# The last feed-forward's second product by Strassen's seven half-block products, token-major

## The chip, the core and the metric

The kernel runs on one core of a Trainium2 chip. Its engines work side by side, each through its own instructions in their order: TensorE (PE, with its weight loads as PEld), VectorE (DVE), ScalarE (ACT), GpSimd (POOL); SyncE (SP) issues most of the loads and stores. The metric is the device time of one execution in microseconds (us), median of several. The span is the time from the first to the last instruction of one profiled execution.

## What is computed

Two transformer-like blocks follow each other on x of 512 tokens by 1024 channels, in fp32. The last step of the second block is the part that is changed; all else (projections, a state-space scan, window attention, a first feed-forward, a recurrent mixer, latent attention, cross attention to a memory) stays.

```python
def rmsnorm_2(x, g):
    xf = x.astype(jnp.float32)
    y = xf * lax.rsqrt(jnp.mean(xf * xf, axis=-1, keepdims=True) + EPS)
    return (y * g.astype(jnp.float32)).astype(x.dtype)
...
        h = rmsnorm_2(x, norm_ffn_g[l])
        x = x + jnp.square(jax.nn.relu(h @ w_ff1[l])) @ w_ff2[l]
    return x
```

w_ff1 is 1024 by 4096, w_ff2 is 4096 by 1024. The factor 1/rms of a token goes through relu and square as 1/rms squared, so the kernel multiplies the result of the second product by 1/(mean of squares + EPS), a number for each token, and uses h without that factor.

## The kernel before

Matrices are held with 128 rows on the partitions. Each fp32 factor of a large product is split into two parts of a narrower type (fp32r): hi, a cast on ScalarE, and lo, source minus hi, on VectorE. A product is three matmuls: hi by hi, lo by hi, hi by lo. Weights come in units of 1 MB (class `Unit`): `load` issues the DMA on SyncE's queue into `raw` (two buffers), `split` makes `whi` (L140) and `wlo` (L141), two buffers each, in two halves of 128x1024. `use(key)` splits the unit that is used and the next one in the stream, and loads the one after that; so the casts of a unit wait until TensorE has read the last matmul of the unit two places ahead of it.

The last feed-forward is `mlp(1, ...)`. It goes over the 4096 hidden channels in four quarters q. In a quarter the first product (keys "f1", four units) makes 8 tiles of 128 hidden channels by 512 tokens, each of 24 matmuls of 128x512 (L267 to L269 of the helper `cm`; the first two units of the first quarter through `cm4`, L1024 to L1026). `f_evac` takes a tile out of PSUM: relu and square on ScalarE (into `ua_h`), the same square in full precision on GpSimd (`fsq`, L1166) and the difference on VectorE (`ua_l`, L1167). The second product (keys "f2", four units) makes 8 tiles of 128 output channels by 512 tokens, each of 24 matmuls again, through two PSUM banks (tag "g") in turn. In the first three quarters its sums gather in `acc` in SBUF; in the last, `fin2` multiplies by the factor of each token (`rb`, spread over the partitions by `bcast_tokens`, L337, from `token_sums`, L330), adds the residual `xT` (channels on the partitions), and `out_channels` turns each finished tile by four transposes (L1703), copies it and stores it token-major.

A scheduler of the framework sets each engine's order within the limits of the data; the engines then keep that order. What sets the order by hand are the lines of `use`, `ahead` and `cm`. The first feed-forward, `mlp(0, ...)`, uses the same function.

## Time and profile before

| | us |
|---|---|
| median of three runs | 1928.96 (1928.72 to 1932.59) |
| the profiled execution's own time | 1931.84 |
| its span | 1930.1 |
| TensorE busy | 1867.0 (97%) |
| VectorE busy | 1046.5 (54%) |
| ScalarE busy | 886.8 (46%) |
| GpSimd busy | 480.3 (25%) |
| mean granted clock of TensorE | 0.994 of full speed |

Busy times are of one profiled execution. Matmuls are pipelined: one of 128x512 shows some 0.39 us from its start to its modelled end, while the next one starts some 0.23 us after it. A wait's releaser is the engine and line that ended it. The difference of 1.74 us between the execution's time and its span lies around the span.

### The profile page before, as it was taken

The numbers are of one execution on the slowest core, as the hardware profiler recorded it, in microseconds if no ns is written. First come the engines' busy times: TensorE is split into PE (matmuls) and PEld (weight loads), VectorE is DVE, ScalarE is ACT, GpSimd is POOL, SyncE is SP. The second block draws the span as 40 slices with busy tenths as digits, with TensorE's granted clock in tenths as the row PEclk, the third lists the DMA queues.
The fourth block names the chain that finished last, engine by engine and source line by source line (L and its number), as shares of the span: only waits on it lengthen the run. The fifth ranks groups of instructions, "written<-read, shape, count | busy, mean of one in ns | idle before, by whom it ended". The sixth has DMA issues, their size and how long they took to land. (4 is left out here: it accounts for less than half of the span.)

```text
span 1930.1 us, 24665 instructions
## 1 busy us (share of the span) xinstructions
PE 1867.0 (97%) x9685; PEld 1541.7 (80%) x9685; DVE 1046.5 (54%) x1687; ACT 886.8 (46%) x1461; POOL 480.3 (25%) x530
## 2 busy tenths in 40 slices
PE   8899999999999999998999999989999999999999
PEld 7788888888887777886888888887867778888887
DVE  6767762666456653547233334667567763333543
ACT  6656663766435664345332323444453543323231
POOL 1454441444202321234021202322111431101020
PEclk9999999999999999999999999999999999999999
DMA  5222112222232222332323223322112213332322
GB/s 170 73 68 68 55 59 88 67 68 63 84 96 83 65 74 88 124 118 93 115 87 111 97 88 109 97 77 68 51 44 66 87 44 109 100 97 88 108 88 66
DMA packets 169378, 164.11 MB, mean 85 GB/s; under 512 B 8742, under 2 KB 165101, under 8 KB 169262
## 3 DMA queue, kind: packets, MB, share of 16 engines
q1 hardware_dynamic: 157322, 151.03, 24.9%
q10 hardware_dynamic: 9444, 9.89, 1.6%
q0 software_dynamic: 2496, 1.61, 0.4%
q8 instruction: 76, 1.25, 0.3%
q14 instruction: 40, 0.33, 0.1%
HBM read 158.26 MB, written 4.23 MB: 84 GB/s over the span
## 5 line engine op out<-in xcount | busy, mean ns | idle before, releaser
L141 DVE TENSOR_TENSOR wlo<-raw,whi 128x1024 fp32r<-128x1024 f32 (+2 forms) x285 | 368.1, 1305 | 272.5 <-ACT whi L140 263.2
L140 ACT CAST whi<-raw 128x1024 fp32r<-128x1024 f32 (+2 forms) x285 | 288.1, 1031 | 412.5 <-PE psg L268 387.8
L267 PE MATMUL psg<-hh,whi 128*128 128x512 f32 (+1 forms) x1016 | 404.0, 398 | 0.8 <-DVE hl L319 0.8
L268 PE MATMUL psg<-hl,whi 128*128 128x512 f32 (+1 forms) x1016 | 401.1, 395 | 0.0
L269 PE MATMUL psg<-hh,wlo 128*128 128x512 f32 (+1 forms) x1016 | 398.8, 393 | 0.0
L267 PE MATMUL psg<-ua_h,whi 128*128 128x512 f32 x800 | 316.5, 396 | 0.5 <-DVE xT L1564 0.5
L268 PE MATMUL psg<-ua_l,whi 128*128 128x512 f32 x800 | 313.4, 392 | 0.0
L269 PE MATMUL psg<-ua_h,wlo 128*128 128x512 f32 x800 | 312.3, 390 | 0.0
L267 PEld LDWEIGHTS psg<-hh,whi 128*128 128x128 f32 (+1 forms) x1016 | 191.0, 188 | 40.7 <-issue 1.2
L269 PEld LDWEIGHTS psg<-hh,wlo 128*128 128x128 f32 (+1 forms) x1016 | 191.0, 188 | 40.0
L268 PEld LDWEIGHTS psg<-hl,whi 128*128 128x128 f32 (+1 forms) x1016 | 191.0, 188 | 38.6 <-DVE hl L316 0.4
L1166 POOL TENSOR_TENSOR fsq<-relu 128x512 f32<-128x512 f32 x64 | 80.9, 1265 | 508.1 <-ACT relu L1163 477.6
L267 PEld LDWEIGHTS psg<-ua_h,whi 128*128 128x128 f32 x800 | 150.0, 188 | 35.3 <-DVE xT L1564 2.4
L268 PEld LDWEIGHTS psg<-ua_l,whi 128*128 128x128 f32 x800 | 150.3, 188 | 32.4 <-DVE ua_l L1167 1.2
L269 PEld LDWEIGHTS psg<-ua_h,wlo 128*128 128x128 f32 x800 | 150.2, 188 | 30.8
L285 PE MATMUL psg<-whi,hh 128*128 128x256 f32 x416 | 122.5, 295 | 10.6 <-ACT cacc L571 3.6
L286 PE MATMUL psg<-wlo,hh 128*128 128x256 f32 x416 | 120.4, 289 | 1.0 <-DVE wlo L141 1.0
L287 PE MATMUL psg<-whi,hl 128*128 128x256 f32 x416 | 120.7, 290 | 0.0
L988 POOL TENSOR_TENSOR ssq<-ssq,sq 128x512 f32<-128x512 f32 x42 | 66.5, 1583 | 117.2 <-ACT sq L987 116.1
L285 PEld LDWEIGHTS psg<-whi,hh 128*128 128x128 f32 x416 | 80.4, 193 | 16.6 <-ACT sz L609 5.8
L1167 DVE TENSOR_TENSOR ua_l<-fsq,ua_h 128x512 fp32r<-128x512 f32 x64 | 47.3, 739 | 79.5 <-POOL fsq L1166 79.5
L286 PEld LDWEIGHTS psg<-wlo,hh 128*128 128x128 f32 x416 | 80.6, 194 | 1.5 <-DVE wlo L141 1.2
(569 smaller groups left out, 2913.4 us busy)
## 6 DMA issues: line engine op xcount, KB each, us to landing
raw<-in_w_in_dram SPq DMA_DIRECT2D x37, 1024.0 KB
raw<-in_w_ff_dram SPq DMA_DIRECT2D x32, 1024.0 KB
raw<-in_w_mlp_in_dram SPq DMA_DIRECT2D x16, 1024.0 KB
raw<-in_w_mlp_out_dram SPq DMA_DIRECT2D x16, 1024.0 KB
raw<-in_w_in_dram SPq DMA_DIRECT2D x16, 512.0 KB
raw<-in_w_ssd_out_dram SPq DMA_DIRECT2D x8, 1024.0 KB
raw<-in_w_attn_out_dram SPq DMA_DIRECT2D x4, 1024.0 KB
raw<-in_w_o_dram SPq DMA_DIRECT2D x4, 1024.0 KB
```

The costliest lines, as they stand in the source:

```text
L140: A.copy(self.hi[sl], self.raw[sl])
L141: V.tensor_tensor(out=self.lo[sl], in0=self.raw[sl], in1=self.hi[sl].bitcast(F32), op=ALU.subtract)
L267: T.matmul(o, lhsT=u.hi[:, k, c:e], rhs=xh[k], start=k == 0, stop=False)
L268: T.matmul(o, lhsT=u.hi[:, k, c:e], rhs=xl[k], start=False, stop=False)
L269: T.matmul(o, lhsT=u.lo[:, k, c:e], rhs=xh[k], start=False, stop=k == u.kt - 1)
L285: T.matmul(o, lhsT=xh[k][:, tk], rhs=u.hi[:, k, 0 : u.n], start=k == 0, stop=False)
L286: T.matmul(o, lhsT=xh[k][:, tk], rhs=u.lo[:, k, 0 : u.n], start=False, stop=False)
L287: T.matmul(o, lhsT=xl[k][:, tk], rhs=u.hi[:, k, 0 : u.n], start=False, stop=k == u.kt - 1)
L988: G.tensor_tensor(out=self.t, in0=self.t, in1=q, op=ALU.add)
L1166: G.tensor_tensor(out=f, in0=r, in1=r, op=ALU.mult)
L1167: V.tensor_tensor(out=ua_l[:, m, :], in0=f, in1=ua_h[:, m, :].bitcast(F32), op=ALU.subtract)
```

## The change

The change replaces the second product of the last feed-forward. In each quarter the product of 512 tokens by 1024 hidden channels with 1024 hidden channels by 1024 outputs is cut into halves in all three directions and done by seven products of half-blocks in place of eight (Strassen's scheme in its variant with shared sums). One half-block product is 256 tokens by 512 hidden channels by 512 outputs: two groups (i) of 12 matmuls of 128x512, tokens on the output's partitions, with the hidden activations as weights and the model's weights as the moving side.

- The weights come as four quads of 1 MB a quarter (`quad`), five buffers with the sum `t3`; `halves` makes their sums and differences on VectorE, and `Made.split` splits the seven that the products need.
- The activations stay in full precision in `ff`; `f_evac` makes their sums and differences on VectorE, `parts` splits one side for each product (`ah` a cast on ScalarE, `al` a subtract on VectorE, 128x1024 each). GpSimd's squares are gone.
- Products 0, 1 and 2 are kept in six PSUM banks (tags e, c, o, y, t) over all four quarters; products 3 to 6 go through the two banks of tag "g" and `gather` adds them in SBUF, to `p6`, `p5` or directly to the residual.
- `seed` turns the residual `xT` in place into token-major form in the first quarter (32 transposes) and multiplies it by mean of squares + EPS of its token; the final `store` multiplies by the inverse. So `rb`, its four transposes and the 32 transposes of `out_channels` are gone.
- In the last quarter `gather` adds the seven products up to the four output blocks on VectorE and `store` scales (ScalarE, the last block also VectorE) and stores.
- `ua_h`, `ua_l` and `acc` are given back before the last feed-forward; the pool of `xT` lies at the other side of SBUF.

```diff
@@ -139,6 +139,19 @@
                     sl = (slice(None), slice(c, e)) if self.flat else (slice(None), slice(None), slice(c, e))
                     A.copy(self.hi[sl], self.raw[sl])
                     V.tensor_tensor(out=self.lo[sl], in0=self.raw[sl], in1=self.hi[sl].bitcast(F32), op=ALU.subtract)
+    class Made(Unit):
+        def __init__(self):
+            super().__init__(4, 512, [])
+        def load(self):
+            pass
+        def split(self):
+            assert self.raw is not None
+            super().split()
@@ -246,8 +259,14 @@
         for q in range(4):
             for u in range(4):
                 plain(("f1", b, q, u), w1, 1024 * q + 256 * u)
-            for u in range(4):
-                plain(("f2", b, q, u), w2, 256 * u, r0=1024 * q)
+            if b == 0:
+                for u in range(4):
+                    plain(("f2", b, q, u), w2, 256 * u, r0=1024 * q)
+            else:
+                for i in range(7):
+                    key = ("s", q, i)
+                    unit_of[key], pos[key] = Made(), len(stream)
+                    stream.append(unit_of[key])
     def cm(key, act, evac, parts=1):
@@ -343,9 +362,11 @@
     mhalf = const([P, 16], "mhalf")
     hh = hp.tile([P, KT, S], F32R, name="hh", tag="hh")
     hl = hp.tile([P, KT, S], F32R, name="hl", tag="hl")
-    ua_h = hp.tile([P, KT, S], F32R, name="ua_h", tag="ua_h")
-    ua_l = hp.tile([P, KT, S], F32R, name="ua_l", tag="ua_l")
-    acc = hp.tile([P, KT, S], F32, name="acc", tag="acc")
+    upper = ExitStack()
+    up = upper.enter_context(tc.tile_pool(name="upper", bufs=1))
+    ua_h = up.tile([P, KT, S], F32R, name="ua_h", tag="ua_h")
+    ua_l = up.tile([P, KT, S], F32R, name="ua_l", tag="ua_l")
+    acc = up.tile([P, KT, S], F32, name="acc", tag="acc")
@@ -960,7 +981,7 @@
     att.close()
-    rp = ctx.enter_context(tc.tile_pool(name="resid", bufs=1, reuse_waits="tile"))
+    rp = ctx.enter_context(tc.tile_pool(name="resid", bufs=1, reuse_waits="tile", side="right"))
@@ -1692,35 +1713,165 @@
     o_dst = out[0].rearrange("(t p) d -> p t d", p=P)
-    outs = []
-    def out_channels(m):
...
-    def last2(m, rb):
...
-    def fin2(m, po, rb):
...
-    mlp(1, xsq, fin2, last=last2)
-    out_channels(KT - 1)
+    upper.close()
+    ff_pool = ctx.enter_context(tc.tile_pool(name="ff", bufs=1, reuse_waits="tile"))
+    def ft(name, shape, bufs=1, dt=F32):
+        return ff_pool.tile(list(shape), dt, name=nm(name), tag=name, bufs=bufs)
+    ff, s3 = ft("ff", (P, KT, S)), ft("s3", (P, 4, 256))
+    low, high = slice(0, 256), slice(256, 512)
+    parts_of = {n: ft(n, (P, 2, S)) for n in ("p1", "p7", "p6", "p5")}
+    ms, r2 = tmp("rtok", (P, NT)), tmp("rtok", (P, NT))
+    def seed():
+        V.tensor_scalar(out=ms, in0=token_sums(xsq.t), scalar1=1.0 / D, scalar2=EPS, op0=ALU.mult, op1=ALU.add)
+        V.reciprocal(out=r2, in_=ms)
+        for k in range(KT):
+            pt = bank("ty"[k % 2])
+            for t in range(NT):
+                T.transpose(pt[:, t * P : t * P + P], xT[:, k, t * P : t * P + P], ident)
+            V.tensor_tensor(out=xT[:, k, :].rearrange("p (t n) -> p t n", t=NT), in0=pt.rearrange("p (t n) -> p t n", t=NT),
+                            in1=ms.unsqueeze(2).broadcast_to([P, NT, P]), op=ALU.mult)
+    def block(name, i):
+        if name[0] == "p":
+            return parts_of[name][:, i, :].rearrange("p (k n) -> p k n", n=P)
+        r, c = int(name[1]) - 1, int(name[2]) - 1
+        t = 2 * r + i
+        return xT[:, 4 * c : 4 * c + 4, t * P : t * P + P]
+    def quad(q, r, c):
+        w = ft("quad", (P, 4, S), bufs=5)
+        nc.sync.dma_start(out=w, in_=kp(a["w_ff2_2"][0][1024 * q + 512 * r : 1024 * q + 512 * r + 512, 512 * c : 512 * c + 512]))
+        return w
+    def halves(op, out, in0, in1):
+        for c in (low, high):
+            V.tensor_tensor(out=out[:, :, c], in0=in0[:, :, c], in1=in1[:, :, c], op=op)
+    def parts(src):
+        h, l = ft("ah", (P, 4, 256), bufs=2, dt=F32R), ft("al", (P, 4, 256), bufs=2, dt=F32R)
+        split_from(src, h, l)
+        return h, l
+    held = {}
+    first, last_ = ff[:, 0:4, low], ff[:, 4:8, low]
+    SIDES = (first, s3, last_, ff[:, 4:8, high], first, ff[:, 0:4, high], last_)
+    SUMS = ("p1", "p7", "c11", "c21", "p6", "p5", "c12")
+    KEPT = {0: "ee", 1: "co", 2: "yt"}
+    def f_evac(m, po):
+        r = tmp("relu")
+        A.activation(r, po, AF.Relu)
+        A.activation(ff[:, m, :], r, AF.Square)
+        if m == 3:
+            held[0] = parts(SIDES[0])
+            V.tensor_tensor(out=s3, in0=first, in1=ff[:, 0:4, high], op=ALU.subtract)
+            held[1] = parts(s3)
+        if m >= 4:
+            j = m - 4
+            V.tensor_tensor(out=ff[:, j, high], in0=ff[:, j, high], in1=ff[:, m, high], op=ALU.add)
+            V.tensor_tensor(out=ff[:, j, low], in0=ff[:, j, high], in1=ff[:, j, low], op=ALU.subtract)
+    def add(y, x):
+        V.tensor_tensor(out=y, in0=x, in1=y, op=ALU.add)
+    def store(name, i):
+        t, c = i + 2 * (name[1] == "2"), 512 * (name[2] == "2")
+        b = block(name, i)
+        for j in range(2 if name == "c12" and i else 1):
+            ks = slice(2 * j, 2 * j + 2) if name == "c12" and i else slice(0, 4)
+            (A.activation(b[:, ks], b[:, ks], AF.Copy, scale=r2[:, t : t + 1]) if name != "c12" or (i and j) else
+             V.tensor_scalar(out=b[:, ks], in0=b[:, ks], scalar1=r2[:, t : t + 1], scalar2=None, op0=ALU.mult))
+            (nc.scalar if j else nc.sync).dma_start(
+                out=o_dst[:, t, c + P * ks.start : c + P * ks.stop].rearrange("p (k n) -> p k n", n=P), in_=b[:, ks])
+    def gather(n, i, po, q):
+        if n in KEPT and q < 3:
+            return
+        name, pv4 = SUMS[n], po.rearrange("p (k n) -> p k n", n=P)
+        if n < 2 or (q == 0 and name[0] == "p"):
+            A.copy(block(name, i), pv4)
+        else:
+            add(block(name, i), pv4)
+        if q < 3:
+            return
+        B = lambda s: block(s, i)
+        if n == 2:
+            add(B("c11"), B("p1"))
+            store("c11", i)
+        elif n == 4:
+            add(B("p6"), B("p1"))
+            add(B("p7"), B("p6"))
+            add(B("c21"), B("p7"))
+            store("c21", i)
+            add(B("c22"), B("p7"))
+            add(B("c12"), B("p6"))
+        elif n == 5:
+            add(B("c12"), B("p5"))
+            add(B("c22"), B("p5"))
+            store("c22", i)
+        elif n == 6:
+            store("c12", i)
+    kept = {}
+    def second(q, w):
+        raws = (w[0, 0], w["t3"], w[1, 0], w[1, 0], w[0, 0], w[0, 1], w[1, 1])
+        for n in range(7):
+            if n < 6:
+                unit_of["s", q, n + 1].raw = raws[n + 1]
+            if n == 2:
+                halves(ALU.subtract, w[1, 0], w[1, 0], w[0, 0])
+                if q < 3:
+                    for i in range(2):
+                        unit_of["f1", 1, q + 1, i].load()
+            u = use(("s", q, n))
+            if 1 <= n < 6:
+                held[n + 1] = parts(SIDES[n + 1])
+            if n == 3:
+                V.tensor_tensor(out=last_, in0=last_, in1=first, op=ALU.subtract)
+            ah, al = held.pop(n)
+            for i in range(2):
+                if n in KEPT:
+                    if q == 0:
+                        kept[n, i] = bank(KEPT[n][i])
+                    o = kept[n, i]
+                else:
+                    o = bank("g")
+                fresh = q == 0 or n not in KEPT
+                ends = q == 3 or n not in KEPT
+                tk = slice(i * P, i * P + P)
+                for k in range(4):
+                    T.matmul(o, lhsT=ah[:, k, tk], rhs=u.hi[:, k, :], start=fresh and k == 0, stop=False)
+                    T.matmul(o, lhsT=al[:, k, tk], rhs=u.hi[:, k, :], start=False, stop=False)
+                    T.matmul(o, lhsT=ah[:, k, tk], rhs=u.lo[:, k, :], start=False, stop=ends and k == 3)
+                gather(n, i, o, q)
+    for q in range(4):
+        w = {(r, c): quad(q, r, c) for r, c in ((0, 0), (1, 1), (0, 1), (1, 0))}
+        w["t3"] = ft("quad", (P, 4, S), bufs=5)
+        unit_of["s", q, 0].raw = w[0, 0]
+        u0 = 0
+        if q == 0:
+            cm4(("f1", 1, 0, 0), ("f1", 1, 0, 1), h_act, f_evac)
+            seed()
+            u0 = 2
+        for u in range(u0, 4):
+            if u == 2:
+                halves(ALU.subtract, w["t3"], w[1, 1], w[0, 1])
+            run(cm(("f1", 1, q, u), h_act, lambda j, po: f_evac(2 * u + j, po)))
+            if u == 2:
+                halves(ALU.subtract, w[0, 1], w[0, 1], w[0, 0])
+        halves(ALU.add, w[0, 0], w["t3"], w[0, 0])
+        second(q, w)
```

VectorE in the last quarter, in the second product. Before: `fin2` (L1719, L1720) and the splits of the units.

```order
L1719 TENSOR_TENSOR acc<-psg_14875,rb_13257 128x512
L1720 TENSOR_TENSOR xT<-xT,acc 128x512
L141 TENSOR_TENSOR wlo_14911<-raw_14846,whi_14910 128x8x128 x2
L1719 TENSOR_TENSOR acc<-psg_14918,rb_13257 128x512
L1720 TENSOR_TENSOR xT<-xT,acc 128x512
```

Now, from the adds for the second half of product 4 to those for product 5 (`psg_15153` and `psg_15171` are the two halves of product 5 in the banks of tag g; p6_, p7_, p5_ and p1_ are the sums of those names in SBUF).

```order
L1784 TENSOR_TENSOR p6_2091_12980<-p1_2089_12978,p6_2091_12980 128x512
L141 TENSOR_TENSOR wlo_2375_15144<-quad_2318_14658,whi_2374_15143 128x4x256
L1784 TENSOR_TENSOR p7_2090_12979<-p6_2091_12980,p7_2090_12979 128x512
L1784 TENSOR_TENSOR xT_6993<-p6_2091_12980,xT_6993 128x4x128
L1784 TENSOR_TENSOR xT_6993<-p7_2090_12979,xT_6993 128x4x128 x2
L335 TENSOR_TENSOR al_2377_15150<-ff_2087_12976,ah_2376_15149 128x1024
L1784 TENSOR_TENSOR p5_2092_12981<-psg_2378_15153,p5_2092_12981 128x512
L1784 TENSOR_TENSOR p5_2092_12981<-psg_2379_15171,p5_2092_12981 128x512
L1784 TENSOR_TENSOR xT_6993<-p5_2092_12981,xT_6993 128x4x128 x4
```

Where two instructions stood between an evacuation and the next, a split, the part of the activations and the adds that finish the blocks now stand ahead of product 5's evacuation.

SyncE's queue at the start of the last feed-forward. Before: four units of w_ff1, then the units of w_ff2.

```order
L129 DMA raw_2043_12722<-in_w_ff1_2_dram 128x8x256
L129 DMA raw_2071_12864<-in_w_ff1_2_dram 128x8x256
L129 DMA raw_2089_12975<-in_w_ff1_2_dram 128x8x256
L129 DMA raw_2104_13107<-in_w_ff1_2_dram 128x8x256
L129 DMA raw_2107_13115<-in_w_ff2_2_dram 128x8x256
```

Now:

```order
L129 DMA raw_2043_12725<-in_w_ff1_2_dram 128x8x256
L129 DMA raw_2071_12867<-in_w_ff1_2_dram 128x8x256
L129 DMA raw_2102_12999<-in_w_ff1_2_dram 128x8x256
L1750 DMA quad_2095_12984<-in_w_ff2_2_dram 128x4x512
L1750 DMA quad_2096_12986<-in_w_ff2_2_dram 128x4x512
L1750 DMA quad_2097_12988<-in_w_ff2_2_dram 128x4x512
L1750 DMA quad_2098_12990<-in_w_ff2_2_dram 128x4x512
L129 DMA raw_2126_13185<-in_w_ff1_2_dram 128x8x256
```

The four quads have moved ahead of the fourth unit of w_ff1.

## Rows read from the trace of the kernel before

**Rows 1.** The page's part 1: busy us, share of the span and instructions of each engine.
```profile
PE 1867.0 (97%) x9685; PEld 1541.7 (80%) x9685; DVE 1046.5 (54%) x1687; ACT 886.8 (46%) x1461; POOL 480.3 (25%) x530
```

**Rows 2.** Windows of the last feed-forward: the first product of the second quarter, its second product, and the second product of the last quarter; us, busy time (and instructions) of PE, PEld, DVE, ACT and POOL, granted clock, DMA share, GB/s.
```profile
1664.00:1708.00 44.00, 44.00 (x196) 36.44 (x195) 16.93 (x16) 16.97 (x24) 10.28 (x8) 1.00 0.30 96
1708.00:1752.00 44.00, 44.00 (x195) 36.27 (x194) 15.23 (x17) 8.03 (x8) 0.00 (x0) 1.00 0.32 98
...
1883.00:1925.00 42.00, 41.74 (x198) 34.29 (x196) 14.88 (x20) 7.49 (x11) 0.00 (x0) 1.00 0.20 63
```

**Rows 3.** The waits of TensorE from 1577 to 1925 us, all of them: who waited for whom, us in total, times, longest.
```profile
PE pse L1026 <- DVE wlo L141: 0.2, 1, 0.2
```

**Rows 4.** The chain that ended last, the first and last of 17 matmuls in a row of a first product, then the token sums and the four transposes of `bcast_tokens`: start, us to the next piece, engine, tile and line.
```profile
1609.89 0.23 PE psg L268
...
1613.52 0.23 PE psg L269
...
1615.10 0.79 PE pst L330 x8
...
1616.71 0.44 PE pst L337 x4
```

**Rows 5.** TensorE's timeline at the end: start, us, and in brackets the idle time before and its releaser.
```profile
1923.91 0.40 PE L269 MATMUL psg<-ua_h,wlo 128*128 128x512 f32 x1
1924.14 0.60 PE L1703 MATMUL pst<-ident,xT 128*128 128x128 f32 x4
1925.57 0.41 PE L1703 MATMUL pst<-ident,xT 128*128 128x128 f32 x2 [0.83 <-DVE xT L1720]
```

**Rows 6.** VectorE's timeline in the last quarter's second product and at the end.
```profile
1888.80 0.69 DVE L1719 TENSOR_TENSOR acc<-psg,rb 128x512 f32<-128x512 f32 x1 [4.04 <-PE psg L269]
1889.52 0.69 DVE L1720 TENSOR_TENSOR xT<-xT,acc 128x512 f32<-128x512 f32 x1
1890.13 2.35 DVE L141 TENSOR_TENSOR wlo<-raw,whi 128x1024 fp32r<-128x1024 f32 x2
...
1924.34 0.76 DVE L1719 TENSOR_TENSOR acc<-psg,rb 128x256 f32<-128x256 f32 x2 [4.52 <-PE psg L269]
```

**Rows 7.** VectorE's groups by form, first from 1620 to 1664 us (GpSimd silent), then from 1664 to 1708 us (GpSimd at its squares): busy us, mean ns of one, idle before and releaser.
```profile
L141 DVE TENSOR_TENSOR wlo<-raw,whi 128x1024 fp32r<-128x1024 f32 x8 | 9.8, 1225 | 33.8 <-ACT whi L140 33.8
...
L141 DVE TENSOR_TENSOR wlo<-raw,whi 128x1024 fp32r<-128x1024 f32 x8 | 12.0, 1501 | 15.9 <-ACT whi L140 15.9
```

**Rows 8.** ScalarE's timeline while a unit is split, and its last copy.
```profile
1627.21 1.05 ACT L140 CAST whi<-raw 128x1024 fp32r<-128x1024 f32 x1 [4.62 <-PE psg L268]
1628.16 0.58 ACT L1171 COPY acc<-psg 128x512 f32<-128x512 f32 x1
1628.64 1.05 ACT L140 CAST whi<-raw 128x1024 fp32r<-128x1024 f32 x1
...
1926.08 0.37 ACT L1705 COPY sq<-pst 128x256 f32<-128x256 f32 x1 [0.67 <-PE pst L1703]
```

**Rows 9.** VectorE's timeline for the same unit.
```profile
1628.29 1.23 DVE L141 TENSOR_TENSOR wlo<-raw,whi 128x1024 fp32r<-128x1024 f32 x1 [8.29 <-ACT whi L140]
1629.72 1.23 DVE L141 TENSOR_TENSOR wlo<-raw,whi 128x1024 fp32r<-128x1024 f32 x1 [0.20 <-ACT whi L140]
```

**Rows 10.** SyncE's queue: the first issue of the last two stores, and what they took.
```profile
1926.47 0.91 SPq L1706 DMA_DIRECT2D out_dram<-sq  x2
```

**Rows 11.** SyncE's queue from 1510 to 1580 us: the first four units of w_ff1, from the first issue to the end of the last.
```profile
1514.94 63.22 SPq L129 DMA_DIRECT2D raw<-in_w_ff_dram  x4
```

**Rows 12.** Windows in which one unit of 1 MB is loaded (last column GB/s).
```profile
1515.00:1520.00 5.00, 5.00 (x23) 3.74 (x21) 1.94 (x9) 1.20 (x4) 1.01 (x1) 1.00 0.71 210
1535.00:1540.00 5.00, 4.95 (x23) 3.42 (x23) 4.03 (x16) 3.15 (x10) 1.86 (x2) 1.00 0.71 210
1560.00:1565.00 5.00, 4.69 (x21) 3.55 (x20) 4.20 (x7) 3.72 (x7) 1.43 (x1) 1.00 0.62 189
1579.00:1585.00 6.00, 6.00 (x28) 4.94 (x27) 0.00 (x0) 0.00 (x0) 0.00 (x0) 1.00 0.56 169
```

**Rows 13.** The end of the split of the second unit of w_ff1 on VectorE, and the first cast of the fourth unit on ScalarE.
```profile
1576.55 1.21 DVE L141 TENSOR_TENSOR wlo<-raw,whi 128x1024 fp32r<-128x1024 f32 x1
...
1593.19 1.04 ACT L140 CAST whi<-raw 128x1024 fp32r<-128x1024 f32 x1
```

**Rows 14.** TensorE's timeline at two long waits early in the kernel, and matmuls after the second.
```profile
78.69 1.65 PE L646 MATMUL pso<-xw,bt 128*128 128x256 f32 x3 [2.93 <-DVE xw L643]
...
93.48 1.10 PE L684 MATMUL psy<-xt,w 128*128 128x64 f32 x8 [2.05 <-DVE xd L699]
...
95.06 0.63 PE L268 MATMUL psg<-hl,whi 128*128 128x512 f32 x1
95.49 0.63 PE L269 MATMUL psg<-hh,wlo 128*128 128x512 f32 x1
95.92 0.63 PE L267 MATMUL psg<-hh,whi 128*128 128x512 f32 x1
```

**Rows 15.** Windows around these waits (the column after POOL is the granted clock).
```profile
75.00:80.00 5.00, 2.07 (x7) 1.41 (x6) 4.68 (x7) 1.43 (x3) 4.77 (x7) 0.77 0.64 171
80.00:85.00 5.00, 5.00 (x14) 3.86 (x14) 4.60 (x8) 0.59 (x1) 1.93 (x3) 0.55 0.22 53
85.00:90.00 5.00, 5.00 (x28) 4.21 (x27) 3.89 (x7) 4.42 (x7) 1.74 (x4) 1.00 0.00 0
...
95.00:100.00 5.00, 5.00 (x21) 4.12 (x20) 3.41 (x7) 3.11 (x4) 4.83 (x8) 0.68 0.01 3
```

19 lines of the change are left out of this document (removed).

## The prediction

> **What bounds the kernel now.** Read the page's busy times first: TensorE is busy 97% of the span, VectorE 54%, ScalarE 46% [rows 1]. Shares over the span can hide stages with other limits, so the windows of the last feed-forward come next: in both kinds of product TensorE fills its window at a granted clock of 1.00, while VectorE works some 15 to 17 of 44 us [rows 2]. The waits confirm it: from 1577 to 1925 us TensorE waits 0.2 us in all [rows 3]. So a matmul that goes is time saved there, one for one, and work for VectorE and ScalarE is free until they come too late. The price of a matmul is the distance from start to start, not its shown duration: in the chain 17 matmuls stand from 1609.89 to 1613.52, 16 distances of 0.227 us [rows 4].
>
> **TensorE's matmuls.** The second product had 4 quarters of 8 tiles of 24 matmuls, 768; now 4 quarters of 7 products of 2 groups of 12, 672. All are of 128x512, so the distance stays. 96 x 0.227 = **21.8 us less**. One product is a step of 24 x 0.227 = 5.45 us.
>
> **Turns and the tail.** The four transposes of `bcast_tokens` go (0.44 us [rows 4]); of the residual's 32 transposes, 28 already stood in TensorE's stream and the last four in the tail, so four come into the stream: these two cancel. The tail from the last matmul's successor at 1924.14 [rows 5] to the span's end at 1930.1 is 6.0 us. In the new one the evacuation comes after 0.20 us as now (1924.14 to 1924.34 [rows 6]), takes 0.72 (L1719 to its dependent L1720 [rows 6]), a half-width scale on ScalarE 0.4 (copy of 128x256 [rows 8]), 0.1 to the issue, and from the last issue to the end 1930.1 - 1926.47 = 3.6 [rows 10]: 5.0. **0.9 us less.**
>
> **The start.** `seed` asks VectorE for the token factor and eight multiplies between the splits, and TensorE's turns wait for two banks in turn. Four quads are now ahead of the fourth unit of w_ff1 on SyncE's queue; a wait there would hold ScalarE's cast of that unit, with the evacuations queued behind it. Before, the fourth unit was issued last, at 1578, alone on the queue [rows 11]. A unit takes about 5 us when it moves alone (210 GB/s for 5 us [rows 12]). The third unit is issued about 1559 (the window from 1560 shows it [rows 12]), the quads behind it need only buffers that cross attention has given back, so four quads and the fourth unit land by 1559 + 6 x 5 = 1589, 4 us ahead of its first cast at 1593.19 [rows 13]; at the 169 GB/s of the last window in rows 12 they would land by 1596 and cost up to 2 us. VectorE waits for the third quad till about 1579 and has four subtracts then, while it has nothing to do after 1577.8 [rows 13]. I take 0.8 us for the hand-overs of the turns, within 0 and 2.3.
>
> **The first three quarters: does VectorE keep up?** Prices: a 1024-wide subtract 1.13 us in a row (two in 2.35, the last 1.22), 1.23 alone; a 512-wide one 0.61 to the next, 0.72 if the next needs its result [rows 6, 9]; a cast 1.05, 0.95 to the next [rows 8]. They are the prices with GpSimd silent; beside its squares the same subtract takes 1,501 ns against 1,225 [rows 7], and GpSimd has nothing left here. A product's split can't begin before TensorE lets go of the buffer two places ahead, which the wait of the cast on L268 shows [rows 8]: at the start of the step before its use. The chain of a step is cast 1.05 + subtracts 1.23 + 1.13 + the activations' subtract 1.13 = 4.5 us plus hand-overs, against 5.45. VectorE's work: products 1 to 2 take 2 x 1.13 + 1.13 for splits and parts; the difference of two quads adds 2.3 behind it, the next step 3.4 + 1.13 for a difference of activations, each later step 3.4 + 2 x 0.61 for evacuations = 4.6. The two heavy steps together take 3.4 + 2.3 + 4.5 = 10.2 of 10.9 us. The place with the least room is the evacuation of product 3's first half, on which the first matmul of product 4 waits through the bank: I find it some 0.1 us early. So these quarters nearly hide. I take 0.3 us each, **1.0 us more**; the lower end is 0, the upper end 6: if every subtract cost the 1,501 ns, a step's three would be 0.84 us longer, 0.35 beyond its slack, in 18 steps.
>
> **The last quarter: it does not.** Here `gather` leaves 14 more adds and the copies of what was kept. From the start of product 1 VectorE has, up to the evacuation that frees a bank for product 6, 18 instructions of 1024 and 19 of 512: 18 x 1.13 + 19 x 0.61 = 31.9, plus 7 that need the result just before, 7 x 0.11 = 0.8, and 1.2 until the first cast is there: 33.9 us. TensorE is through products 1 to 5 after 5 x 5.45 = 27.2. Product 6 starts **6.7 us late**, whatever part of it shows as earlier waits; by my walk through the order 0.3 before product 2, 1.5 before product 4, 0.3 in product 5 and 4.6 before product 6. The Trainium skill (VectorE: DVE Perf Modes, section on the TRN2 errata) prices such an instruction as a fixed part and its width, 594 ns for 512 columns from SBUF, 658 from PSUM and 1,127 for 1024. By it the list would come to 0.7 us less.
>
> **The clock.** After such a wait TensorE's clock comes down. Early in the kernel it stood 2.93 us and 2.05 us [rows 14]; after the first the clock was lowered for 0.23 x 2 x 5 + 0.45 x 2 x 5 = 6.8 us, after the second 0.32 x 2 x 5 = 3.2 us [rows 15], at matmuls 0.43 us apart [rows 14], which is the 1.2 GHz level. A wait of 4.6 us is nearer to the longer one, of whose 6.8 us some 2.3 fall into the wait itself: 4.5 us at half speed lose 2.2. I take **2.0 us more**, within 0 and 3.4.
>
> **The sum.** -21.8 - 0.9 + 0.8 + 1.0 + 6.7 + 2.0 = -12.2 us. From the profiled execution's 1931.84 that is 1919.6; that execution lay 2.9 us above the median of the runs, so the median becomes 1928.96 - 12.2 = **1916.8 us**.
>
> **The rivals.**
> - *Slower: the steps of all quarters are paced by VectorE's chain.* If splits, activation part and both evacuations follow one another from the step's start, a step is 1.05 + 1.23 + 1.13 + 1.13 + 0.61 + 0.69 = 5.84 us and three hand-overs of 0.2 (L140 to the second subtract in rows 9 shows one), 6.4 in place of 5.45: 0.95 x 18 = 17 us, and the clock falls in three more quarters, 3 x 2.0. 1916.8 - 1.0 + 17 + 6 = 1939. It ends slower once an ordinary step loses more than (12.2 + 1.0) / 18 = 0.73 us. Against it: evacuation and split overlap on two engines, and the sums above fit into the step.
> - *The clock falls in every quarter.* Short waits at product 4 or at the seams add up until the clock comes down, 1.7 to 3.4 us a time, in three more quarters: 1922 to 1927, about 1924. For it: 2.05 us of waiting was enough once [rows 14]. Against it: I find no ordinary wait above a few tenths. The Trainium skill (TensorE: Matmul & The Clock Gate, section HAM oscillation) tells of a kernel whose short bursts between waits each start on the lowered clock. No row of this stage shows such waits [rows 3].
> - *The last quarter hides better.* No clock loss, no waits at the start or in the first quarters, the list 0.7 us shorter: 1916.8 - 2.0 - 0.8 - 1.0 - 0.7 = 1912.3. Without any wait at all it would be 1928.96 - 22.7 = 1906.3, which the list of 33.9 us forbids.
>
> **How the numbers follow.** Forecast (1914 to 1920) 0.60; hides better (1910 to 1914) 0.18; clock in every quarter (1920 to 1927) 0.12; slower by VectorE's chain 0.07; other mishaps 0.03. The range of 8 in 10 runs from 1910.5, the better case with most of its spread, to 1924.5, the middle of the clock case. About 0.2% (3.9 us) is what a measurement of this kernel can tell from no change: below 1925.1 lies the forecast, the better case and most of the clock case, 0.87; within, 0.06; above 1932.8, the slow case, 0.07.
>
> **What would show it.** Right: L1853 to L1855 at distances of 0.227 us, 672 of them; TensorE's waits below 1 us in each of the first three quarters, then several us on VectorE's `p5` and `xT` adds (L1784), the longest ahead of the last product; the subtracts of weights near 1,225 ns; clock 1.00 until that wait and lower in the last 10 us. Wrong: waits of TensorE on `wlo` or `al` in all quarters, a wait of ScalarE or VectorE for a quad or for the fourth unit of w_ff1, or subtracts well above 1.23 us although GpSimd is silent.

## The result and the profile after

| | us |
|---|---|
| before, median of 5 runs | 1929.55 (1928.72 to 1932.59) |
| changed, median of 5 runs | 1918.1 (1912.72 to 1921.17) |
| ratio, 95% interval | 0.9937 [0.9918, 0.9955], 12.2 us less |
| predicted | 1916.8, range 1910.5 to 1924.5 |
| changed, the profiled execution and its span | 1921.17, span 1919.1 |

The change makes the kernel faster by about the amount forecast. Part 1 of the page of the changed kernel, beside [rows 1]: TensorE stays the bound, VectorE has taken work over, GpSimd has given some up.

```profile
PE 1845.2 (96%) x9585; PEld 1522.5 (79%) x9585; DVE 1135.2 (59%) x1784; ACT 937.7 (49%) x1511; POOL 439.6 (23%) x498
```

The stages are what to compare, and TensorE's timeline gives them: each begins with its first matmul. These are the first matmuls of the first products, of the second product of the first quarter and of the one of the last quarter (start, us).

```profile
1573.65 0.47 PE L1045 MATMUL psg<-hh,whi 128*128 128x512 f32 x1
...
1623.09 0.39 PE L1853 MATMUL pse<-whi,ah 128*128 128x512 f32 x1
...
1868.10 0.39 PE L1853 MATMUL pse<-whi,ah 128*128 128x512 f32 x1
```

Read so for both kernels (last matmul's end: its start plus 0.227 us):

| stage | before: start, length | changed: start, length | difference |
|---|---|---|---|
| first quarter, first products | 1570.04, 45.71 | 1573.65, 49.44 | +3.73 |
| first quarter, second product | 1615.75, 44.12 | 1623.09, 38.13 | -5.99 |
| second quarter, first | 1659.87, 43.52 | 1661.22, 43.52 | 0 |
| second quarter, second | 1703.39, 43.62 | 1704.74, 38.16 | -5.46 |
| third quarter, first | 1747.01, 43.52 | 1742.90, 43.52 | 0 |
| third quarter, second | 1790.53, 43.59 | 1786.42, 38.16 | -5.43 |
| last quarter, first | 1834.12, 43.52 | 1824.58, 43.52 | 0 |
| last quarter, second | 1877.64, 46.50 | 1868.10, 46.14 | -0.36 |
| tail, to the span's end | 1924.14, 5.96 | 1914.24, 4.86 | -1.10 |
| the last feed-forward | 360.06 | 345.45 | -14.61 |

So the stage gained 14.6 us, more than the 12.2 of the whole kernel: in this execution it began 3.6 us later, though the instructions ahead of it are the same. That difference is looked into below.

Windows of the same stages (columns as in [rows 2]): a first product, the second product of the second quarter, and that of the last quarter.

```profile
1661.22:1704.74 43.52, 43.52 (x194) 36.05 (x192) 19.65 (x22) 17.98 (x25) 0.00 (x0) 1.00 0.31 95
1704.74:1742.90 38.16, 38.16 (x170) 31.48 (x168) 32.97 (x34) 19.78 (x22) 0.00 (x0) 1.00 0.32 114
1868.10:1914.24 46.14, 40.60 (x169) 32.17 (x167) 39.60 (x48) 23.84 (x29) 0.00 (x0) 0.96 0.12 37
```

In an ordinary quarter TensorE fills the window at full clock although VectorE works 33.0 of 38.2 us. In the last one it does not. Its waits from 1574 us to the end, all of them (as [rows 3]):

```profile
PE psg L1853 <- DVE p L1784: 4.1, 1, 4.1
PE psg L1853 <- DVE xT L1784: 1.5, 1, 1.5
PE psg L1045 <- DVE xT L1585: 0.5, 1, 0.5
PE pse L1047 <- DVE wlo L141: 0.2, 1, 0.2
```

The lower two were there before (at 1571.65 and 1577.82 us of the other trace, 0.45 and 0.19). The upper two stand ahead of products 4 and 6 of the last quarter. VectorE's timeline there, from product 4's evacuation on, shows what the last product waited for:

```profile
1895.36 0.68 DVE L1784 TENSOR_TENSOR p<-psg,p 128x512 f32<-128x512 f32 x1
1896.08 1.42 DVE L1784 TENSOR_TENSOR p<-p,p 128x512 f32<-128x512 f32 x2
1897.41 1.89 DVE L1784 TENSOR_TENSOR xT<-p,xT 128x512 f32<-128x512 f32 x3
...
1903.30 1.88 DVE L1784 TENSOR_TENSOR xT<-p,xT 128x512 f32<-128x512 f32 x3
1905.10 1.21 DVE L335 TENSOR_TENSOR al<-ff,ah 128x1024 fp32r<-128x1024 f32 x1
1906.24 1.28 DVE L1784 TENSOR_TENSOR p<-psg,p 128x512 f32<-128x512 f32 x2
1907.44 2.48 DVE L1784 TENSOR_TENSOR xT<-p,xT 128x512 f32<-128x512 f32 x4
```

TensorE had finished product 5 at 1902.8. The evacuation of its first half (the first of the two at 1906.24) frees the bank of product 6, and stands behind the ten finishing adds of product 4, the evacuation of its second half and the splits of the last product's weights and activations (the rows left out hold that evacuation, two of the adds and the weights' two halves). TensorE's timeline behind that wait:

```profile
1902.59 0.39 PE L1855 MATMUL psg<-wlo,ah 128*128 128x512 f32 x1
1907.06 0.47 PE L1853 MATMUL psg<-whi,ah 128*128 128x512 f32 x1 [4.08 <-DVE p L1784]
...
1908.99 0.63 PE L1853 MATMUL psg<-whi,ah 128*128 128x512 f32 x1
1909.41 0.63 PE L1854 MATMUL psg<-whi,al 128*128 128x512 f32 x1
...
1914.01 0.39 PE L1855 MATMUL psg<-wlo,ah 128*128 128x512 f32 x1
```

At 1909 us the matmuls stand 0.43 us apart: the clock is at its lower level, 1.2 GHz, and comes back before the end. Product 6 takes 1914.24 - 1907.06 = 7.18 us in place of 5.45. The subtract of weights with GpSimd silent has the shorter of the two prices of [rows 7], as the page shows:

```profile
L141 DVE TENSOR_TENSOR wlo<-quad,whi 128x1024 fp32r<-128x1024 f32 x56 | 67.1, 1220 | 45.2 <-ACT whi L140 45.2
```

### The profile page after: what moved, and what is told of

The parts are those of the page before. It is cut to its first block, busy times and chain, and to the rows that moved or that the text cites. A ratio compares the mean times of both kernels' runs of the same rounds, so it can differ in the third digit from the quotient of the medians.

```text
span 1919.1 us, 24498 instructions
## 1 busy us (share of the span) xinstructions
PE 1845.2 (96%) x9585; PEld 1522.5 (79%) x9585; DVE 1135.2 (59%) x1784; ACT 937.7 (49%) x1511; POOL 439.6 (23%) x498
## 5 line engine op out<-in xcount | busy, mean ns | idle before, releaser
L141 DVE TENSOR_TENSOR wlo<-raw,whi 128x1024 fp32r<-128x1024 f32 (+3 forms) x253 | 321.6, 1286 | 228.8 <-ACT whi L140 224.7
L140 ACT CAST whi<-raw 128x1024 fp32r<-128x1024 f32 (+3 forms) x253 | 254.7, 1028 | 295.6 <-PE psg L287 255.8
L286 PE MATMUL psg<-ua_h,whi 128*128 128x512 f32 x544 | 216.1, 398 | 0.6 <-DVE xT L1585 0.6
L287 PE MATMUL psg<-ua_l,whi 128*128 128x512 f32 x544 | 213.5, 392 | 0.0
L288 PE MATMUL psg<-ua_h,wlo 128*128 128x512 f32 x544 | 212.6, 391 | 0.0
L286 PEld LDWEIGHTS psg<-ua_h,whi 128*128 128x128 f32 x544 | 102.0, 188 | 25.6 <-DVE xT L1585 2.4
L287 PEld LDWEIGHTS psg<-ua_l,whi 128*128 128x128 f32 x544 | 102.3, 188 | 22.1 <-issue 1.0
L288 PEld LDWEIGHTS psg<-ua_h,wlo 128*128 128x128 f32 x544 | 102.2, 188 | 20.7
L141 DVE TENSOR_TENSOR wlo<-quad,whi 128x1024 fp32r<-128x1024 f32 x56 | 67.1, 1220 | 45.2 <-ACT whi L140 45.2
L140 ACT CAST whi<-quad 128x1024 fp32r<-128x1024 f32 x56 | 57.1, 1049 | 71.7 <-PE psg L287 32.9
```

What stands on the lines that cost most here:

```text
L140: A.copy(self.hi[sl], self.raw[sl])
L141: V.tensor_tensor(out=self.lo[sl], in0=self.raw[sl], in1=self.hi[sl].bitcast(F32), op=ALU.subtract)
L286: T.matmul(o, lhsT=u.hi[:, k, c:e], rhs=xh[k], start=k == 0, stop=False)
L287: T.matmul(o, lhsT=u.hi[:, k, c:e], rhs=xl[k], start=False, stop=False)
L288: T.matmul(o, lhsT=u.lo[:, k, c:e], rhs=xh[k], start=False, stop=k == u.kt - 1)
```

## The experiments

Ratios are to the kernel before on the same chip; lengths are read from the traces as above (last feed-forward: from its first matmul to the span's end). One trace repeats another's stages well: the changed kernel twice gave 345.45 and 345.44, the kernel before 360.06 and 359.98. A difference of 0.2 us in a stage is therefore meaningful, while a median of the whole kernel is not to be read closer than some 3 us.

| kernel | median, us | ratio, 95% | last feed-forward | its last second product | tail |
|---|---|---|---|---|---|
| changed | 1918.1 | 0.9937 [0.9918, 0.9955] | 345.45 | 46.14 | 4.86 |
| e1 free banks | 1917.75 | 0.9926 [0.9912, 0.9941] | 344.38 | 45.00 | 4.85 |
| e2 adds late | 1915.96 | 0.9918 [0.9903, 0.9934] | 343.57 | 39.92 | 9.22 |
| e3 no finishing adds | 1910.63 | 0.9900 [0.9876, 0.9924] | 337.72 | 38.44 | 4.81 |
| e4 subtract twice | 1928.56 | 0.9980 [0.9970, 0.9990] | 355.58 | 46.12 | 4.86 |
| e5 shorter list | 1913.78 | 0.9906 [0.9891, 0.9920] | 338.84 | 38.48 | 5.13 |
| e6 squares on GpSimd | 1918.02 | 0.9929 [0.9915, 0.9944] | 346.56 | 46.71 | 4.89 |
| e7 plain products | 1931.47 | 1.0001 [0.9989, 1.0013] | 359.81 | 43.52 | 5.61 |
| e8 no turn | 1915.37 | 0.9911 [0.9895, 0.9928] | 342.81 | 47.25 | 4.85 |
| e9 changed, again | 1920.04 | 0.9936 [0.9917, 0.9955] | 345.44 | 46.11 | 4.85 |
| e10 shorter list, again | 1912.65 | 0.9896 [0.9881, 0.9910] | 338.88 | 38.48 | 5.14 |
| e11 before, again (one run) | 1929.95 | | 359.98 | 46.49 | 5.92 |
| e12 sum on VectorE | 1908.85 | 0.9886 [0.9868, 0.9905] | 338.87 | 38.49 | 5.11 |

### e1: the bank, or what stands ahead of it?

```diff
-                    o = bank("g")
+                    o = bank("g" if q < 3 or n < 5 else {5: "co", 6: "yt"}[n][i])
```

> Theory: in the last quarter VectorE's list is what is late, not the bank. With free banks for the last two products the wait for the evacuation goes, but the last product still needs its activations' low half (al), which stands behind the same ten adds and is done some 0.6 us before that evacuation was: TensorE waits about 3.5 us on al in place of 4.1 on p5, the clock still falls, the last quarter goes from 46.1 us to about 45.5 and the time by 0.6 us, to about 1917.5. Rival: the bank is what is late. Then both the wait and the fall of the clock go: the last quarter is 39.6 us, the time about 1911.7.

TensorE's timeline at its longest wait in e1:

```profile
1902.21 0.50 PE L1854 MATMUL psy<-whi,al 128*128 128x512 f32 x1 [3.20 <-DVE al L335]
```

VectorE's timeline there:

```profile
1900.94 1.21 DVE L335 TENSOR_TENSOR al<-ff,ah 128x1024 fp32r<-128x1024 f32 x1
1902.08 0.68 DVE L1784 TENSOR_TENSOR p<-psc,p 128x512 f32<-128x512 f32 x1
```

With the banks free, the wait is 3.2 us, now for `al`, and the clock still falls. The bank was only the first of the things behind the adds; freeing it brought 1.1 us of the stage.

### e2: the same adds, later

```diff
-        elif n == 4:
-            add(B("p6"), B("p1"))
...
+        elif n == 5 and i:
+            for i in range(2):
+                add(B("p6"), B("p1"))
...
```

> Theory: the ten adds behind product 4 only stand in the way; put behind product 5's evacuations they leave al of the last product done at about 1901.4 us, ahead of product 5's end at 1902.8. The wait before the last product and the fall of the clock go (6.4 us of the last quarter, 46.1 to 39.7), but VectorE's list is as long as before: it now ends behind the last matmul, the tail grows from 4.9 to about 7.5 us, and the time falls by some 3 to 4 us, to about 1914.5. Rival: hand-overs, not the adds, make the wait; then it stays near 4 us and the time at 1918.

The wait before product 6 and the fall of the clock are gone (39.92 us; the 1.5 us before product 4 stay), so the adds it was. But the list is as long as before, and it comes out at the other end. TensorE's last matmul in e2:

```profile
1904.05 0.39 PE L1855 MATMUL psg<-wlo,ah 128*128 128x512 f32 x1
```

VectorE's last work:

```profile
1903.86 3.09 DVE L1784 TENSOR_TENSOR xT<-p,xT 128x512 f32<-128x512 f32 x5
...
1907.98 0.35 DVE L1792 TENSOR_SCALAR xT<-xT,rtok 128x256 f32<-128x256 f32 x1
```

The window behind the last matmul (columns as above, the last one GB/s):

```profile
1904.00:1913.50 9.50, 0.43 (x2) 0.01 (x1) 4.30 (x8) 1.84 (x3) 0.00 (x0) 0.69 0.48 143
```

VectorE ends 4 us behind TensorE, and from there to the span's end it is 5.2 us in place of the changed kernel's 3.6, with five stores issued within 1.7 us. That the bunched stores are the reason is not shown: in e7 below the last stores are spread as in the changed kernel, and it is 4.35 us there. The tail is 1.7 us longer than I expected; of 6.2 us saved 4.4 are given back.

### e3: no finishing adds

```diff
-            add(B("c11"), B("p1"))
...
-            add(B("p6"), B("p1"))
-            add(B("p7"), B("p6"))
-            add(B("c21"), B("p7"))
...
```

> Leaves out the sixteen adds that combine the products' sums at the end (c11 to c22 are stored without them). Theory: the list up to the evacuation that frees the bank shrinks from 33.9 us by 14 x 0.61 = 8.5 to 25.4, below TensorE's 27.2: no wait before the last product, 0.3 us or less before product 4, no fall of the clock; last quarter 38.2 to 38.5 us, tail as now, time about 1910.3. Rival: the splits and hand-overs of the steps make the waits; then several us of them stay and the time lies near 1915 to 1918.

No wait of TensorE is left behind 1612 us, the last second product takes 38.44 us, 0.3 more than an ordinary one, and the tail stays. So the finishing adds cost 46.14 - 38.44 = 7.7 us, fall of the clock included, and hand-overs 0.3 at most.

### e4: how much room do the other quarters have?

```diff
         split_from(src, h, l)
+        if again:
+            V.tensor_tensor(out=l, in0=src, in1=h.bitcast(F32), op=ALU.subtract)
...
-                held[n + 1] = parts(SIDES[n + 1])
+                held[n + 1] = parts(SIDES[n + 1], q < 3)
```

> In the second products of the first three quarters VectorE does each subtract of the activations' split twice, 1.13 us more in each of six steps. Theory (sums of the prediction: two heavy steps 10.2 of 10.9 us, later ones 4.6 of 5.45): the heavy two become 12.5, 1.6 us too long, the later ones 0.3 each: about 2.5 us of waits a quarter, 7.5 in three, time about 1925.6, more if the clock falls. Rival, no slack (the chain of a step is the pace): 18 x 1.13 = 20 us, about 1938. Rival, more slack than I counted: no wait, time 1918.

Neither rival holds: the three second products take 41.96, 41.31 and 41.33 us, 10.2 us more in all, for 3 x 6.8 us of added work. The theory's 7.5 was too little. TensorE's waits in e4 from 1612 us on, those that the changed kernel has not:

```profile
PE psy L1856 <- DVE al L1761: 2.5, 3, 0.8
PE psg L1856 <- DVE al L1761: 2.2, 5, 0.6
...
PE psg L1855 <- ACT p L1803: 1.2, 1, 1.2
```

VectorE's timeline at the first wait of the second quarter, the second of the two subtracts:

```profile
1718.99 1.22 DVE L1761 TENSOR_TENSOR al<-ff,ah 128x1024 fp32r<-128x1024 f32 x1
```

TensorE's timeline there:

```profile
1719.05 0.39 PE L1855 MATMUL pst<-whi,ah 128*128 128x512 f32 x1
1720.27 0.50 PE L1856 MATMUL psy<-whi,al 128*128 128x512 f32 x1 [0.82 <-DVE al L1761]
```

The matmul on `al` of product 2 starts 1720.27 - 1719.05 = 1.22 us after its neighbour in place of 0.23: 0.99 us late for 1.13 us of added work. The room there was 0.14 us. The whole quarter had some 3.6 us (6.8 added, 3.2 lost), but the tightest place had almost none, and it is this split, not the evacuation of product 3 where the prediction looked for it.

### e5 and e10: a shorter list

```diff
+        w["t4"] = ft("quad", (P, 4, S), bufs=6)
...
+        halves(ALU.subtract, w["t4"], w[1, 0], w[0, 0])
...
+            if q == 3 and u < 2:
+                for y, x in ("c12", "p6"), ("c21", "p6"), ("c22", "p6"), ("c12", "p5"), ("c22", "p5"):
+                    add(block(y, u), block(x, u))
...
-            if n == 3:
-                V.tensor_tensor(out=last_, in0=last_, in1=first, op=ALU.subtract)
+            if n == 0:
+                V.tensor_tensor(out=s3, in0=last_, in1=first, op=ALU.subtract)
...
+                    o = bank("yt"[i] if q == 3 and n == 5 else "g")
```

In `gather` of the last quarter, c11, c21 and c22 take what PSUM kept straight from the banks, product 4 is added onto a copy of product 0, and c12 and c22 take product 5 from its bank.

> VectorE's work in the last quarter is cut and moved, the matmuls stay as they are: the three quarters' sums p6 and p5 are added into c12, c21 and c22 while the last first product runs, what PSUM kept of products 0 and 1 is added from the bank, the two differences stand ahead of the second product, product 5 has banks of its own. In the window that leaves 22 adds of 512 in place of 26 and takes three subtracts of 1024 out: 4 x 0.61 + 3 x 1.13 = 5.8 us less, a list of 28.1 us or less to the last product's operands, beside 27.2 of TensorE, with most adds behind them. Theory: no wait before the last product nor before product 4, no fall of the clock, last quarter 38.2 to 38.8 us, tail 4.9 to 6, time 1910 to 1911.5. Rival: as in the kernel with the late adds, the work only moves behind the last matmul; then the tail is 8 to 9 us and the time 1914.

The window of e5's last second product:

```profile
1867.99:1906.47 38.48, 38.37 (x169) 31.27 (x167) 36.22 (x44) 22.67 (x27) 0.00 (x0) 1.00 0.11 35
```

VectorE's timeline at its end:

```profile
1899.39 1.22 DVE L335 TENSOR_TENSOR al<-s,ah 128x1024 fp32r<-128x1024 f32 x1
1900.53 1.28 DVE L1784 TENSOR_TENSOR xT<-psy,xT 128x512 f32<-128x512 f32 x2
...
1904.13 1.28 DVE L1784 TENSOR_TENSOR xT<-p,xT 128x512 f32<-128x512 f32 x2
...
1907.39 0.35 DVE L1792 TENSOR_SCALAR xT<-xT,rtok 128x256 f32<-128x256 f32 x1
```

`al` of the last product is done at 1900.6, just ahead of the end of product 5 (1906.47 - 5.45 = 1901.0), and the remaining adds run beside product 6; the last of the finishing ones ends at 1905.4, before it does. The kernel makes several moves at once (adds earlier, adds straight from the banks, differences earlier, banks of its own for product 5), and what each brings was not separated. The last feed-forward is 6.6 us shorter than the changed kernel's, though the splits of the first three quarters cost it 0.4, 0.2 and 0.2 us. Its medians of 1913.78 and 1912.65 lie 4 to 7 us below the changed kernel's; the second time on the same chip as e9:

> The kernel with the shorter list once more, on the same chip as the changed kernel. By its stages (338.9 us against 345.5) it lies 6.6 us below the changed kernel, of which 5.5 are the two waits, 2.1 the fall of the clock, less 0.8 at the splits of the first three quarters and 0.3 in the tail; ratio about 0.989 to 0.991 to the kernel before. Rival: what it saves in the last quarter is lost elsewhere; then the two are within 2 us.

Measured there: 1912.65 against 1920.04, with the same stages as the first time. What the last quarter saves is not lost elsewhere.

### e6: the squares back on GpSimd

```diff
-        A.activation(ff[:, m, :], r, AF.Square)
+        G.tensor_tensor(out=ff[:, m, :], in0=r, in1=r, op=ALU.mult)
```

> The squares of the activations go back to GpSimd, nothing else changes. Theory: VectorE's subtracts beside them take about 1.5 us in place of 1.22, in first products where it has over 20 of 43.5 us to spare, so the time stays within 1 us of 1918.1 and no wait of TensorE over 0.5 us appears at the seams. Rival: leaving GpSimd out is part of the gain; the later squares and slower subtracts come late at the start of the second products, waits of 1 to 2 us in each quarter, time 1922 to 1926.

VectorE's groups by form in e6, in the first product of the second quarter:

```profile
L141 DVE TENSOR_TENSOR wlo<-raw,whi 128x1024 fp32r<-128x1024 f32 x6 | 7.8, 1313 | 15.6 <-ACT whi L140 15.6
...
L335 DVE TENSOR_TENSOR al<-s,ah 128x1024 fp32r<-128x1024 f32 x1 | 2.1, 2067 | 0.0
```

The subtracts beside GpSimd's squares are longer, one takes 2,067 ns in place of 1,225, and the second products of the first three quarters still take 38.11, 38.17 and 38.16 us. The start is 0.5 us longer (49.96), the clock behind the wait of 4.1 us stayed down longer in this trace. Leaving GpSimd out is no part of the gain that can be measured.

### e7: token-major with plain products

```diff
-        raws = (w[0, 0], w["t3"], w[1, 0], w[1, 0], w[0, 0], w[0, 1], w[1, 1])
-        for n in range(7):
+        raws = (w[0, 0], w[1, 0], w[0, 1], w[1, 1])
+        for n in range(4):
+            c, s = divmod(n, 2)
...
+                po = [[bank(t) for t in p] for p in (("ee", "co"), ("gg", "yt"))[c]]
+            for r in range(2):
+                ah, al = held[s, r]
```

> The second product token-major, with the residual turned at the start, but with the eight plain half-block products: 768 matmuls, no sums of blocks. Theory: the gain is the 96 matmuls alone. By stages 49.4 for the first products of the first quarter with the turns, 3 x 43.5 for the other first products, 4 x 43.6 for the second ones without a wait, tail 4.9: 359.2 us against 360.1 before, so within 1 us of the kernel before, ratio about 0.9995. Rival: the layout carries part of the gain (or costs something); then it stands 3 us or more away from the kernel before.

The windows of its first and last second product:

```profile
1622.85:1666.37 43.52, 43.52 (x193) 36.04 (x192) 16.55 (x17) 11.03 (x13) 0.00 (x0) 1.00 0.30 97
1883.97:1927.49 43.52, 43.52 (x193) 35.85 (x191) 14.77 (x16) 13.24 (x16) 0.00 (x0) 1.00 0.13 39
```

The last feed-forward takes 359.81 us against 360.06, the ratio is 1.0001. The layout alone is worth nothing; the 96 matmuls are the gain, and the finishing adds a price that only Strassen's sums bring.

### e8: no turn at the start

```diff
-            pt = bank("ty"[k % 2])
-            for t in range(NT):
-                T.transpose(pt[:, t * P : t * P + P], xT[:, k, t * P : t * P + P], ident)
```

> Leaves out the 32 transposes of the residual (it is scaled where it stands, so the sums start from untransposed values). Theory: the start pays 32 x 0.104 = 3.3 us for the transposes, as the kernel before paid for 28 in its last quarter, and about 0.4 us for hand-overs; without them the first quarter's first products take 45.7 us in place of 49.4, time 3.7 us less, 1914.4. Rival: the prediction's price of 0.8 us for the hand-overs, then 4.1 us less; or the turns lie beside other work of TensorE's and nothing is gained.

The first products of the first quarter take 45.79 us in place of 49.44: 3.65 us for the turn. In the kernel before 28 transposes made a second product of 46.50 us out of 43.60 (its other quarters) or 43.52 (e7), 0.104 to 0.106 us each. 32 of them are 3.3 to 3.4, so the hand-overs cost 0.2 to 0.3 us. By the ratios of the whole kernels it is 5 us; their intervals overlap, and the scatter that comes next is in them.

### e9, e11 and e12: where the rest went

> The changed kernel once more. By stages of the traces so far the last feed-forward became 14.6 us shorter (360.06 to 345.45), while the medians differ by 11.5 us and the ratio gives 12.2. Theory: the rest is the part ahead of it, whose instructions are the same and whose time scatters with falls of the clock (the last feed-forward began between 1569.3 and 1573.7 us in nine traces); then the stage is 345.5 within 1 us again, and the ratio over more runs moves towards 0.9925. Rival: the change makes the part ahead 2 to 3 us slower for good; then its start stays near 1573.6 and the ratio at 0.9937.

> The kernel before once more, for the start of its last feed-forward. Theory of scatter: between 1569 and 1574 us, wherever the clock falls between 1230 and 1270 us and near 1530 us; the last feed-forward 360.1 us long again. Rival: it begins at 1570.0 each time, and only the changed kernels come later.

The stage repeats to 0.1 us and the start of the last feed-forward moves: 1565.56 in e9, 1568.22 in e11, up to 1573.65 over fourteen traces. So the part ahead scatters, and a delay in every execution is out: the earliest start is the changed kernel's own. A delay in most is not, for e9's trace is the fastest of its six runs. But the ratio did not move as the theory had it (0.9936). In the six runs of e9 the span goes from 1911.0 us at a mean clock of 0.998 to 1925.6 at 0.988. Of the 8.1 us between the starts in the two traces of the changed kernel 4.0 stand already at 832 us; the other 4.1 arise around one place. TensorE's wait there in the first trace:

```profile
PE pst L349 <- POOL ssq L1009: 1.9, 1, 1.9
```

And in e9:

```profile
PE pst L349 <- POOL ssq L1009: 0.8, 1, 0.8
```

The window from 1230 us in the first trace (the third number from the end is the granted clock):

```profile
1230.00:1245.00 15.00, 13.09 (x84) 12.89 (x83) 6.36 (x9) 5.11 (x7) 3.38 (x2) 0.77 0.20 56
```

And in e9:

```profile
1230.00:1245.00 15.00, 13.98 (x115) 13.74 (x115) 11.81 (x16) 8.34 (x14) 4.36 (x4) 1.00 0.50 161
```

The timelines of VectorE and of GpSimd there in the first trace:

```profile
1231.50 2.35 DVE L141 TENSOR_TENSOR wlo<-raw,whi 128x1024 fp32r<-128x1024 f32 x2
```

```profile
1232.61 2.36 POOL L1009 TENSOR_TENSOR ssq<-ssq,sq 128x512 f32<-128x512 f32 x1 [4.31 <-ACT sq L1008]
```

The same two in e9:

```profile
1227.54 3.46 DVE L141 TENSOR_TENSOR wlo<-raw,whi 128x1024 fp32r<-128x1024 f32 x2
```

```profile
1228.65 1.27 POOL L1009 TENSOR_TENSOR ssq<-ssq,sq 128x512 f32<-128x512 f32 x1 [4.31 <-ACT sq L1008]
```

In the first trace VectorE's second subtract goes through and GpSimd's add takes 1.1 us longer; in e9 it is the other way. TensorE waits for GpSimd's add. After 1.9 us of waiting its clock falls, after 0.8 it does not. The same holds over the other traces: 1.9 us and a fall of the clock near 1235 in the changed kernel's first, e5, e7 and e8, 0.8 and none there in the other nine, e12's aside. e12 takes the race out, on top of the shorter list:

```diff
-        def add(self, src):
+        def add(self, src, E=G):
...
-                G.tensor_tensor(out=self.t, in0=self.t, in1=q, op=ALU.add)
+                E.tensor_tensor(out=self.t, in0=self.t, in1=q, op=ALU.add)
...
-        ssq.add(acc[:, m, :])
+        ssq.add(acc[:, m, :], V if m == 7 else G)
```

> The kernel with the shorter list, and far ahead of it, near 1235 us, the last of the eight adds of the squares (ssq, L1009) on VectorE, between the two halves of a weight subtract, in place of GpSimd beside them. In the traces so far TensorE waits there 0.8 us when GpSimd's add takes 1.3 us and 1.9 us when it takes 2.4 (it then stands beside a subtract of VectorE's), and the clock falls for 3.4 to 6.8 us right behind the longer wait alone. Theory: the two cases are a race of the two engines, and their mixture is the scatter ahead of the last feed-forward. With the add in VectorE's own order the wait is below 0.6 us, no fall near 1235, the last feed-forward begins below 1570, the median 1 to 3 us below the shorter list's 1913, ratio about 0.9885. Rival: the falls come from elsewhere; then the scatter and the median stay, ratio 0.990.

The wait is gone, and in the window of e12 the clock stands at 1.00:

```profile
1228.00:1245.00 17.00, 17.00 (x140) 16.72 (x138) 13.28 (x19) 9.46 (x16) 2.69 (x2) 1.00 0.41 127
```

The last feed-forward begins at 1568.63, the median is 1908.85 (1907.87 to 1909.34), 3.8 to 4.9 below the shorter list's two medians. All four of its runs lie below all eight of the shorter list's, though the intervals of the ratios overlap. So e12 is faster, but that the race accounts for all of it is not shown. Against e12's trace, e5's, with the wait of 1.9 us, loses 3.3 us between 832 and 1238 us, and e10's, with the wait of 0.8, only 0.6 to 1.0. Yet in e10 the last feed-forward begins as late as in e5 (1572.92 and 1572.76), since its clock stayed down longer at a later place. The window from 1255 us in e10:

```profile
1255.00:1270.00 15.00, 11.39 (x65) 10.56 (x64) 7.99 (x9) 2.38 (x4) 4.66 (x5) 0.77 0.22 67
```

And in e12:

```profile
1255.00:1270.00 15.00, 13.60 (x102) 13.10 (x103) 8.25 (x11) 5.16 (x10) 4.80 (x5) 0.89 0.14 42
```

That is 6.8 us of lowered clock against 3.4, and 2.9 us between the two traces. So the race is one source of the scatter, not the only one. e12's kernel is faster than the one before by some 23 us (on the same chip) and than the changed one by some 9 to 11.

## Why the prediction was right

**The bound and the 21.8 us.** Right and shown. The second and third quarters lost 5.46 and 5.43 us where a product of 5.45 went (the first, which also lost its four transposes of `bcast_tokens`, 5.99), and with 768 matmuls in the same layout (e7) nothing is left of the gain.

**Turns and tail.** The tail went from 5.96 to 4.86 us, 1.1 less against 0.9 in the sum.

**The start.** Taken at 0.8 us, measured 0.3: by the table of stages 3.73 more at the start, 2.90 less for the 28 transposes of the last quarter (46.50 - 43.60) and 0.54 less for those of `bcast_tokens`. e8 agrees with its 0.2 to 0.3. No engine waited for a quad or for the fourth unit of w_ff1 in a way that TensorE felt.

**The first three quarters.** Taken at 1.0, measured 0.0: no wait at all between 1623 and 1868 us. That VectorE keeps up was right; where it is tight was not. The prediction named the evacuation of product 3; e4 shows `al` of product 2, with 0.14 us of room.

**The last quarter.** The forecast was 0.3, 1.5, 0.3 and 4.6 us of waits before products 2, 4, 5 and 6; the trace has 1.46 before product 4 and 4.08 before product 6, and elsewhere up to there no two matmuls more than 0.35 us apart from start to start. From product 1's start at 1873.54 to product 6's at 1907.06 it is 33.5 us, against a list of 33.9: product 6 starts 6.3 us late in place of 6.7. By the formula of the Trainium skill (VectorE: DVE Perf Modes, section on the TRN2 errata) the list is an estimated 0.7 us shorter, 33.2, and the trace lies between the two. The formula's higher price for an add from PSUM, an estimated 658 ns, does not hold here: in the changed kernel's trace such adds of 512 stand 0.60 us apart, as those from SBUF do (the two at 1906.24). That the list and not the bank, nor hand-overs, makes the wait is shown by e1, e2 and e3 together.

**The clock.** Taken at 2.0, here 7.18 - 5.45 = 1.7 us. The working misread one row: of the 6.8 us of lowered clock early in the kernel it put 2.3 into the wait, but in that trace the clock fell at 77.7 us and the wait ended at 78.69, so 1.0 did, and the same reasoning would have given 2.9. That 2.0 came close is in part luck: after the wait of 4.1 us the clock was down for 3.4 us only. In e8, behind the same wait of 4.1 us, the last second product took 1.1 us longer (47.25), in e6 0.6: how long the clock stays down after one and the same wait varies. The Trainium skill's short bursts on a lowered clock (TensorE: Matmul & The Clock Gate, section HAM oscillation) did not appear in the ordinary quarters, where the clock stands at 1.00.

**The sum.** -21.8 for the matmuls, -1.1 tail, +0.3 for the turns, 0.0, +8.0 for the last quarter make -14.6, as the trace says; the forecast was -12.2. The mis-sized terms are the start (0.3 in place of 0.8), the first quarters (0.0 in place of 1.0), the last quarter with its clock (8.0 in place of 8.7) and, by 0.2, the tail, all to the same side. The median is nevertheless 1.3 us above the forecast, because the part ahead gave some 3 us back; so the number came closer than its terms did, by luck. The prediction had no term for that: it took the part ahead as equal. An estimate, each run's span less its kernel's last feed-forward (with 1.8 us around the span where only the time is on record), puts the start of that stage at a median of 1570.7 us in the five changed runs and at 1567.7 in the five before, but at 1570.1 in the 44 other runs of the kernel before and at 1572.8 in e9's six. So in the result most of the 3 us is five low runs of the kernel before; whether the changed kernel is some 1 us later for good is open. What makes the scatter ahead is shown in part, for one place; the falls of the clock near 1260 us (in twelve of fourteen traces) and near 1530 (in six) were not tested.

**The rivals.** That VectorE paces all quarters falls with e4: the changed kernel's first quarters have no wait, and with 1.13 us more in each step they lose half of it. The clock did not fall in every quarter. That the last quarter hides better did not come by itself, but e5 shows that it could be made to.
